# Retention's sample states weighted by their queries before a sum by ones, in units 2 to 7 of a decoder layer

## The chip, the cores and the metric

The kernel runs on one core of a Trainium2 chip. TensorE multiplies matrices, VectorE, ScalarE and GpSimd compute elementwise, and SyncE (SP) issues nearly all DMAs from one queue, in order. The metric is the device time of one execution in microseconds, 2566.4 as the median of three runs (2565.67 to 2569.12).

## The reference

One layer of a decoder trunk, for 16 + 256 prompt tokens and 8 sample tokens (one new token for each of eight sequences with states from the past): a SwiGLU half step, a mixer of Retention (8 heads of 256 by 256) and HGRN2 (16 heads of 128 by 128) behind one input projection of ten parts, an output projection, and a second half step. What the change touches is Retention's output for the sample tokens:

```python
def retention_chunk(S, q, k, v):          # C = 1 for a sample
    ...
    q_dec = q * jnp.exp(lg[:, None] * (idx + 1.0))[:, :, None].astype(q.dtype)
    o = jnp.einsum('bhij,bhjv->bhiv', inner, v) + jnp.einsum('bhid,bhdv->bhiv', q_dec, S)
    ...
    S_new = jnp.exp(lg * C)[:, None, None].astype(S.dtype) * S + jnp.einsum('bhjd,bhjv->bhdv', k_dec, v)
```

For one token, gamma times S plus k times v is the new state, and the output is the query times that new state. So for each head and each of the eight samples b, `o[b, :] = sum over d of q[b, d] * S_new[b, d, :]`, with d over 256, which the kernel holds as two halves c of 128 partitions.

## The kernel before

All matmuls with weights are written three times in fp32r (high by high, low by high, high by low) by `dense` (L218). `stream` loads 512 KB of weights into `raw` (L185, on SP), ScalarE rounds them to `whi` (L188), VectorE subtracts to get `wlo` (L189); each has three buffers of eight weight blocks. TensorE's instructions keep the order in which the program writes them. The other engines' orders are planned ahead by a scheduler that fills them by priority and readiness; after that every queue runs in its order.

The mixer runs over eight units u (a Retention head and two HGRN2 heads each). `project` makes the unit's six parts f, q_h, i_h, q_r, k_r, v_r, then the four gate groups of the unit before. A group is 16 steps k of six matmuls. After each step the hook calls `pump`, which counts down every waiting thread by one and lets those at zero run to their next `yield n`. So a unit has 160 steps, and a thread's position is counted in pumps.

- `mix_hg(u)` starts 4 pumps after i_h. It works off the decay levels (tiles K, Q, T, Qm), updates the sample states (`smh`), and for u of 2 or more waits 45 pumps, until pump 91 of its count, for its query matmuls (`pq`, L1039). After 7 pumps more come `outputs(0)`, then twice 10 for the two norms.
- `mix_ret(u)` starts 3 pumps after v_r, which is 48 pumps after i_h. `load(0)` and `load(1)` (L1095) fetch the states of samples 0 to 3 and 4 to 7 (e = 0, 1), two halves c each, in four buffers with the tag `smr`, which the tiles ks and vs share. `alone(qdr, q)` (L734) spreads the eight queries over a zeroed tile so that a 32-column weight holds one query. L1192 and L1198 update the states in place, L1202 writes them out. At pump 43 the visit of TensorE comes: `scores` for the last prompt tokens, then 16 matmuls (L1211) over e, c and the four column tiles j into `pq` (named pqr). 7 pumps later follow the two output matmuls (`por`), one pump each, and 12 pumps after the last of them the norm's sums (`pvr`), at pump 64.

Pump 43 of `mix_ret` and pump 91 of `mix_hg` are the same pump, so both visits follow each other.

`gate_groups(u)` come after the next unit's parts. The evacuation of a gate (`evacuate`, L690 to L705) calls `pump` without any dense step until the norm of its unit is done (`done_r`, `done_h`). For the last unit its own gate groups come right after those of unit 6: the first of them ends 80 pumps after v_r.

`st` is the dictionary through which `evacuate` hands tiles to the threads. `qdr` is a tile of 4 x 129 columns that holds nothing but Retention's queries.

Of the kernel before, what the change touches and what calls it, by code (L numbers as in the profile page):

```python
# [13 lines left out]
AF = mybir.ActivationFunctionType  # L14
ALU = mybir.AluOpType
# [8 lines left out]
NMETA, SEQ, NS = 16, 256, 8  # L24
# [104 lines left out]
def trunk(ctx: ExitStack, tc: tile.TileContext, A, O):  # L129
    nc = tc.nc  # L130
# [108 lines left out]
    def mul(out, a, b):  # L239
        nc.vector.tensor_tensor(out=out, in0=a, in1=b, op=ALU.mult)  # L240
# [306 lines left out]
    with tc.tile_pool(name="yp", bufs=1) as yp:  # L547
# [7 lines left out]
        with tc.tile_pool(name="mp", bufs=1) as mp:  # L555
# [28 lines left out]
            st = {}  # L584
# [7 lines left out]
            nc.gpsimd.memset(qdr, 0.0)  # L592
            qdh_at = [qdh.rearrange("p a c -> p (a c)")[:, 256 * h :] for h in range(2)]
            qdr_at = [qdr.rearrange("p a c -> p (a c)")[:, 2 * ALONE * c :] for c in range(2)]
            vsm = tmp("vsm", (P, P))
# [52 lines left out]
            def evacuate(n, c0, c1, o0, o1, b0, b1):  # L648
# [38 lines left out]
                elif n in ("g_r", "g_h"):  # L687
# [4 lines left out]
                    sa = tmp("gs", (P, TL), bufs=2)  # L692
                    nc.scalar.activation(sa, o1, AF.Sigmoid)
                    mul(t, t, sa)
                    u, e = divmod(c0, 2)
# [50 lines left out]
            def mix_hg(u, f, k, q, v):  # L746

                calm = 2
# [282 lines left out]
                if u == 1:  # L1031
                    yield 2
                    samples(1)
                yield (8, 11, 45)[min(u, 2)]
                pq = mx_bank("pq")
# [49 lines left out]
            def mix_ret(u, q, k, v):  # L1085
# [6 lines left out]
                def load(e):  # L1092
                    for c in range(2):
                        sms.append(tmp("smr", (P, 4, 256), bufs=4))
                        nc.sync.dma_start(sms[2 * e + c], A["sr"][u, c, :, 4 * e : 4 * e + 4, :])  # L1095

# [7 lines left out]
                for c in range(2):  # L1104
# [27 lines left out]
                    yield 2  # L1132
                alone(qdr, q)
                vts = [vt[:, 0], vt[:, 1], vs2]
# [54 lines left out]
                for e in range(2):  # L1189
# [13 lines left out]
                    yield 1 if e else 10 if u == 0 else 6  # L1203
                yield (11 if u == 0 else 15) + 2 * calm
                pq = mx_bank("pqr")
                scores(pq[:, 256:], 2)
                for e in range(2):
                    for c in range(2):
                        for j in range(4):
                            b = 4 * e + j  # L1210
                            nc.tensor.matmul(  # L1211
                                pq[32 * j : 32 * j + 32, :256], qdr_at[c][:, 32 * b : 32 * b + 32],
                                sms[2 * e + c][:, j, :], start=e + c == 0, stop=e + c == 2, tile_position=(0, 32 * j))
                mul(scr2[:NB2], pq[:NB2, 256 : 256 + NMETA], dt[:NB2, c2:])
# [162 lines left out]
```

## Time and profile before

| what | value |
|---|---|
| median of three runs | 2566.4 us (2565.67 to 2569.12) |
| span of the profiled execution | 2563.9 us |
| TensorE's granted clock in it | 1.000 |
| one unit, from the first pj_f of unit 3 to that of unit 4 in the windows view | 126.3 us |
| VectorE busy in that unit | 98.5 us |
| ScalarE busy in that unit | 84.7 us |
| GpSimd busy in that unit | 6.2 us |
| state loads `smr` from issue to landing, median | 5.0 us |
| weight loads of the input projection, median | 4.3 us |

The span runs from the first to the last instruction; the time of a run lies a little above it. Busy time of an engine is the union of its instructions. A row of a group says the line of the source, the engine, the operation, the tiles (out, then in), the shape and the count, then busy time and the mean duration of one, then the idle time ahead of them and what ended it. A row of the timeline begins with the start and the duration in us. A row of the tile view has the shortest, median and longest duration in ns after the count. A row of the waits view says who waited for whom: total, times, longest.

### The profile page before, as it was taken

To read this page: it belongs to the slowest core of one execution; us is meant where nothing else is said; L and a number is where in the kernel's file an instruction comes from. 1 tells how busy PE (TensorE), PEld (TensorE's weight loads), DVE (VectorE), ACT (ScalarE), POOL (GpSimd) and SP (SyncE) were. 2 spreads that over 40 slices of the span, in tenths; PEclk is the share of its full clock that TensorE was granted. 3 is DMA by queue.
4 is the path that set the end of the run, shared out by engine and by line. 5 is a ranking of instruction groups with operands and counts; after the bars stand their busy time and mean duration, and the time that the engine had idled before them with its cause. 6 is when DMAs were issued, how large, how long until landed. Compare 5 with 4: busy or idle time off the path is not lost.

```text
span 2563.9 us, 56275 instructions
## 1 busy us (share of the span) xinstructions
PE 2553.4 (100%) x23424; PEld 2534.4 (99%) x23424; DVE 1702.8 (66%) x2827; ACT 1392.2 (54%) x2186; POOL 57.0 (2%) x152
## 2 busy tenths in 40 slices
PE   9999999999999999999999999999999999999999
PEld 9999999999999999999999999999999999999998
DVE  6444544475569878777777777777885555556555
ACT  5444444444456767767676666675564444444443
POOL 0000000000000000000000000000000000000000
PEclk9999999999999999999999999999999999999999
DMA  7555555555555876767676767675556565565554
GB/s 244 183 187 183 187 182 184 186 182 186 184 201 180 287 265 232 264 214 260 212 264 215 259 223 255 224 239 188 196 190 197 194 197 195 194 196 195 195 195 149
DMA packets 156897, 536.26 MB, mean 209 GB/s; under 512 B 17952, under 2 KB 25952, under 8 KB 156640
## 3 DMA queue, kind: packets, MB, share of 16 engines
q1 hardware_dynamic: 156352, 532.37, 62.0%
q8 instruction: 183, 3.00, 0.5%
q14 instruction: 74, 0.61, 0.1%
q10 hardware_dynamic: 288, 0.29, 0.0%
HBM read 501.99 MB, written 30.61 MB: 208 GB/s over the span
## 4 chain that ended last, share of the span: by engine, by line
PE 96%; DVE 2%; ACT 0%; issue 0%; DMA 0%; SPq 0%; ACTq 0%; DVEq 0%
PE up L218 36%; PE dn L218 19%; PE pj_i_h L218 3%; PE pj_g_r L218 3%; PE pj_q_h L218 3%; PE pj_g_h L218 3%; PE pj_a_r L218 3%; PE pj_a_h L218 3%; PE pj_f L218 3%; PE pj_q_r L218 3%; PE pj_k_r L218 3%; PE wo L218 3%; PE pj_v_r L218 3%; DVE wlo L189 1%; PE pqr L1211 1%; PE psr L1168 0%
## 5 line engine op out<-in xcount | busy, mean ns | idle before, releaser
L189 DVE TENSOR_TENSOR wlo<-raw,whi 128x1024 fp32r<-128x1024 f32 (+1 forms) x869 | 1062.2, 1223 | 740.7 <-ACT whi L188 737.3
L188 ACT CAST whi<-raw 128x1024 fp32r<-128x1024 f32 (+1 forms) x870 | 905.7, 1042 | 909.2 <-PE up L218 411.0
L218 PE MATMUL up<-xh,whi 128*128 128x280 f32 (+1 forms) x2624 | 725.6, 280 | 0.6 <-ACT whi L188 0.6
L218 PE MATMUL up<-xh,wlo 128*128 128x280 f32 (+1 forms) x2624 | 725.8, 280 | 0.4 <-DVE wlo L189 0.3
L218 PE MATMUL up<-xl,whi 128*128 128x280 f32 (+1 forms) x2624 | 725.4, 279 | 0.0
L218 PEld LDWEIGHTS up<-xh,wlo 128*128 128x128 f32 x2624 | 492.6, 189 | 1.0 <-DVE wlo L189 1.0
L218 PEld LDWEIGHTS up<-xh,whi 128*128 128x128 f32 x2624 | 492.6, 189 | 0.8 <-ACT whi L188 0.8
L218 PEld LDWEIGHTS up<-xl,whi 128*128 128x128 f32 x2624 | 492.6, 189 | 0.0
L218 PE MATMUL dn<-hh,whi 128*128 128x280 f32 (+1 forms) x1376 | 384.7, 280 | 0.0
L218 PE MATMUL dn<-hh,wlo 128*128 128x280 f32 (+1 forms) x1376 | 384.3, 279 | 0.0
L218 PE MATMUL dn<-hl,whi 128*128 128x280 f32 (+1 forms) x1376 | 384.3, 279 | 0.0
L218 PEld LDWEIGHTS dn<-hh,whi 128*128 128x128 f32 x1376 | 260.1, 189 | 0.1
L218 PEld LDWEIGHTS dn<-hl,whi 128*128 128x128 f32 x1376 | 260.1, 189 | 0.1
L218 PEld LDWEIGHTS dn<-hh,wlo 128*128 128x128 f32 x1376 | 260.1, 189 | 0.0
L218 PE MATMUL pj_k_r<-xh,whi 128*128 128x280 f32 x256 | 74.2, 290 | 0.0
L218 PE MATMUL pj_g_r<-xh,whi 128*128 128x264 f32 x256 | 74.0, 289 | 0.0
L218 PE MATMUL pj_v_r<-xh,whi 128*128 128x280 f32 x256 | 73.8, 288 | 0.0
L218 PE MATMUL pj_v_r<-xh,wlo 128*128 128x280 f32 x256 | 72.4, 283 | 0.3 <-DVE wlo L189 0.3
L218 PE MATMUL pj_g_h<-xh,whi 128*128 128x264 f32 x256 | 72.7, 284 | 0.0
L218 PE MATMUL pj_k_r<-xh,wlo 128*128 128x280 f32 x256 | 72.4, 283 | 0.0
L218 PE MATMUL pj_v_r<-xl,whi 128*128 128x280 f32 x256 | 72.3, 283 | 0.0
L218 PE MATMUL pj_k_r<-xl,whi 128*128 128x280 f32 x256 | 72.3, 283 | 0.0
(421 smaller groups left out, 5263.4 us busy)
## 6 DMA issues: line engine op xcount, KB each, us to landing
raw<-in_w_up SPq DMA_DIRECT2D x343, 512.0 KB, 4.1
raw<-in_w_in SPq DMA_DIRECT2D x320, 512.0 KB, 4.3
raw<-in_w_dn SPq DMA_DIRECT2D x172, 512.0 KB, 3.5
smr<-in_sr SPq DMA_DIRECT2D x32, 512.0 KB, 5.0
out_srs<-smr SPq DMA_DIRECT2D x32, 512.0 KB, 6.7
raw<-in_w_out SPq DMA_DIRECT2D x32, 512.0 KB, 3.9
vbr<-vrd SPq DMA_DIRECT2D x32, 256.0 KB, 4.1
smh<-in_sg SPq DMA_DIRECT2D x16, 512.0 KB, 5.2
```

The costliest lines, as they stand in the source:

```text
L188: nc.scalar.copy(hi[:, j:jn, :], raw[:, j:jn, :])
L189: nc.vector.tensor_tensor(out=lo[:, j0:j1, :], in0=raw[:, j0:j1, :], in1=hi[:, j0:j1, :].bitcast(F32), op=ALU.subtract)
L218: nc.tensor.matmul(o, w, t, start=start, stop=stop)
L1211: nc.tensor.matmul(pq[32 * j : 32 * j + 32, :256], qdr_at[c][:, 32 * b : 32 * b + 32], sms[2 * e + c][:, j, :], start=e + c == 0, stop=e + ...
```

## The change

In units 2 to 7 the states are multiplied by the queries outside TensorE: for each sample b and the halves c, `s0 = s0 * q0`, then `s0 = s1 * q1 + s0`, per partition. The matmul then sums over the partitions with a weight of 32 columns in which one column is 1 (`one`), so the loop over c runs once. `one` and `late_q`, the eight queries of both halves, lie in `qdr`. The products for e = 0 are made on GpSimd, those for e = 1 on ScalarE, and the second step of both on VectorE. A GpSimd copy of one column of `st["seen"]`, the sigmoid of the gate evacuated last, stands ahead of the copy of the queries. The products are issued at pump 49 of `mix_ret` and the visit at pump 65; the wait in `mix_hg` grows from 45 to 67. The first two state loads of units 2 to 7 get a GpSimd copy ahead of them that reads a column of `st["q"]`, the HGRN2 queries of the unit, and writes into the buffer. Units 0 and 1 stay as they were.

```diff
+            one = qdr[:, 0, :64].rearrange("p (e m) -> p e m", e=2)
+            late_q = qdr[:, 1, : 2 * NS].rearrange("p (c b) -> p c b", c=2)
...
                     nc.scalar.activation(sa, o1, AF.Sigmoid)
+                    st["seen"] = sa
...
-                yield (8, 11, 45)[min(u, 2)]
+                yield (8, 11, 67)[min(u, 2)]
...
                         sms.append(tmp("smr", (P, 4, 256), bufs=4))
+                        if e == 0 and u > 1:
+                            nc.gpsimd.tensor_copy(sms[c][:, 0, :1], st["q"][:, 0, :1])
                         nc.sync.dma_start(sms[2 * e + c], A["sr"][u, c, :, 4 * e : 4 * e + 4, :])
...
-                alone(qdr, q)
+                if u < 2:
+                    alone(qdr, q)
...
-                yield (11 if u == 0 else 15) + 2 * calm
+                yield (11 if u == 0 else 15) + 2 * calm if u < 2 else 25
+                if u == 2:
+                    nc.gpsimd.memset(qdr[:, 0, :64], 0.0)
+                    for e in range(2):
+                        nc.gpsimd.memset(one[:, e, e : e + 1], 1.0)
+                if u > 1:
+                    nc.gpsimd.tensor_copy(late_q[:, 0, :1], st["seen"][:, :1])
+                    nc.gpsimd.tensor_copy(late_q, q[:, :, SEQ:])
+                    for e in range(2):
+                        s0, s1 = sms[2 * e : 2 * e + 2]
+                        for b in range(4):
+                            g = [late_q[:, c, 4 * e + b : 4 * e + b + 1] for c in range(2)]
+                            if e:
+                                nc.scalar.activation(s0[:, b, :], s0[:, b, :], AF.Copy, scale=g[0])
+                            else:
+                                nc.gpsimd.tensor_scalar(out=s0[:, b, :], in0=s0[:, b, :], scalar1=g[0], scalar2=None, op0=ALU.mult)
+                            nc.vector.scalar_tensor_tensor(
+                                out=s0[:, b, :], in0=s1[:, b, :], scalar=g[1], in1=s0[:, b, :], op0=ALU.mult, op1=ALU.add)
+                    yield 16
                 pq = mx_bank("pqr")
                 scores(pq[:, 256:], 2)
                 for e in range(2):
-                    for c in range(2):
+                    for c in range(2 if u < 2 else 1):
                         for j in range(4):
                             b = 4 * e + j
                             nc.tensor.matmul(
-                                pq[32 * j : 32 * j + 32, :256], qdr_at[c][:, 32 * b : 32 * b + 32],
-                                sms[2 * e + c][:, j, :], start=e + c == 0, stop=e + c == 2, tile_position=(0, 32 * j))
+                                pq[32 * j : 32 * j + 32, :256], qdr_at[c][:, 32 * b : 32 * b + 32] if u < 2 else one[:, e, :],
+                                sms[2 * e + c][:, j, :], start=e + c == 0, stop=e + c == 2 if u < 2 else e == 1, tile_position=(0, 32 * j))
```

## The prediction, made before the changed kernel ran

> **What bounds the kernel now.** I read the page's engine totals first, then the chain that ended last, then TensorE's waits.
>
> ```profile
> span 2563.9 us, 56275 instructions
> ...
> PE 2553.4 (100%) x23424; PEld 2534.4 (99%) x23424; DVE 1702.8 (66%) x2827; ACT 1392.2 (54%) x2186; POOL 57.0 (2%) x152
> ...
> PE 96%; DVE 2%; ACT 0%; issue 0%; DMA 0%; SPq 0%; ACTq 0%; DVEq 0%
> ...
> PE pw L515 <- DVE eps_h L163: 1.0, 1, 1.0
> PE pt L1116 <- POOL tails L1103: 0.9, 1, 0.9
> PE pj_f L218 <- DVE wlo L189: 0.7, 1, 0.7
> ```
>
> The reader is to see that TensorE is the chain (96%), and that its longest single wait on another engine is 1.0 us. Busy alone proves little, since matmuls are pipelined; the three rows of the waits view prove it. So a matmul that goes is time that goes, and any wait that is put into TensorE's queue is time that comes, one for one.
>
> **What goes: half of the query matmuls of units 2 to 7.** These rows are TensorE's timeline at the visit of unit 5 (start, duration, engine, line), and then the grouped row for all eight units.
>
> ```profile
> 1444.27 0.42 PE L1211 MATMUL pqr<-smr,qdr 128*32 128x256 f32 x3
> ...
> 1444.32 1.89 PE L1211 MATMUL pqr<-smr,qdr 128*32 128x256 f32 x29
> 1446.14 0.38 PE L218 MATMUL pj_g_r<-xh,whi 128*128 128x264 f32 x1
> ...
> 1445.59 0.40 PE L1211 MATMUL pqr<-smr,qdr 128*32 128x256 f32 x4
> ...
> 1445.81 0.40 PE L1211 MATMUL pqr<-smr,qdr 128*32 128x256 f32 x4
> ...
> L1211 PE MATMUL pqr<-smr,qdr 128*32 128x256 f32 x256 | 15.5, 381 | 0.0
> ```
>
> A unit has 16 matmuls of L1211 in the source and 32 records (256 / 8): float32 goes through twice. The four column tiles run side by side, so records start in groups of four. The first group's four start between 1444.27 and 1444.32, the eighth's at 1445.81: seven steps of 0.213 to 0.220 us, and I take 0.216 (the two rows of four alone give 0.22). The mean of 381 ns is therefore not the price; the step is. With the loop over c cut to one pass, 4 of 8 groups go: 4 x 0.216 = 0.86 us a unit, and 6 units make **5.2 us**. What surrounds the groups stays: the scores, the gap of about 0.3 us before the next dense matmul (1445.81 to 1446.14), and the float32 weights of 32 columns, which have the same shape whether they hold queries or ones. A cruder reading bounds it from below: 32 starts in 1.56 us are 0.050 us each, 16 of them 0.80 us, 4.8 us in all.
>
> **What comes, part by part.** Per unit: two small GpSimd copies (one waits for the gate's sigmoid), four GpSimd products of 128x256, four ScalarE products, eight VectorE folds; VectorE's small copy of the queries (L734) goes. They are issued 49 pumps after v_r, and the matmuls that read them at 65, where they were issued at 43. One pump is one k step of a projection.
>
> ```profile
> L1198 DVE SCALAR_TENSOR_TENSOR smr<-vbr,k_r,smr x64: 459/479/494, 839.5 to 1683.5; 128x256 f32<-128x256 f32 x64
> L998 ACT ACTIVATE smh<-smh,meta x128: 384/387/410, 866.7 to 1661.7; 128x128 f32<-128x128 f32 x128
> L1192 ACT ACTIVATE smr<-smr,gam x16: 1132/1147/1152, 838.2 to 1677.8; 128x1024 f32<-128x1024 f32 x16
> ...
> L1174 POOL TENSOR_SCALAR gam<-sro x8: 280/1172/1307, 832.2 to 1675.5; 128x1 f32<-128x1 f32 x8
> L592 POOL MEMSET qdr<- 128x516 f32 x1 | 0.5, 532 | 0.0
> ...
> 1448.83 0.28 PE L218 MATMUL pj_a_r<-xh,wlo 128*128 128x264 f32 x1
> ...
> 1449.39 0.28 PE L218 MATMUL pj_a_r<-xl,whi 128*128 128x264 f32 x1
> ...
> 1450.70 0.39 ACT L693 ACTIVATE gs<-pj_a_r 128x264 f32<-128x264 f32 x1
> ...
> 1449.10:1460.60 11.50, 11.50 (x102) 11.40 (x101) 7.16 (x15) 6.47 (x14) 0.00 (x0) 1.00 0.81 289
> ...
> POOL meta L910 <- DVE T L240: 298.6, 5, 59.9
> ```
>
> The row with a colon in its first field is of the windows view: length, then busy us (count) of PE, PEld, DVE, ACT and POOL, the clock, the DMA share and GB/s.
>
> VectorE: 8 x 0.48 = 3.8 us. ScalarE: 128 columns take 0.39, 1024 take 1.15, so 256 take about 0.48 (estimate), 1.9 us in four. GpSimd has no product of this size in the trace. From below: 0.28 us, the shortest TENSOR_SCALAR, of one column. To it I add 256 columns at the memset's rate, 532 / 516 = 1.03 ns each, 0.26 us, and take **0.54 us**. From above: a memset only writes; a product at twice its rate would take 0.8 us, and the wait below comes on top.
>
> The room: the sigmoid that releases the copies ends at 1451.1, 1.6 us after its group's last step (the dense work after pump 43 begins at 1446.14; five steps of six matmuls, 0.56 / 5 = 0.112 us each by the two PE rows, end at 1449.5). From there to pump 65 there are 16 steps of 0.675 us and one of 0.71 us (280 columns for 264), 11.5 us; 9.9 us remain after the sigmoid. Two copies (0.2 us each), four products each followed by its fold, and the four other folds beside ScalarE's products need 0.4 + 4 x 0.54 + 8 x 0.48 = 6.4 us even in a row, with about four weight subtractions (wlo) of 1.2 us between them. VectorE was busy 7.16 of 11.5 us in this window (third pair), and the query tails that stand there move out. So I cost the added work at nothing on TensorE; its cover is those 17 dense steps.
>
> How far VectorE may fall behind is seen where nothing disturbs:
>
> ```profile
> 1733.74 1.05 ACT L188 CAST whi<-raw 128x1024 fp32r<-128x1024 f32 x1 [1.65 <-PE pj_a_h L218]
> ...
> 1734.82 1.23 DVE L189 TENSOR_TENSOR wlo<-raw,whi 128x1024 fp32r<-128x1024 f32 x1 [1.13 <-ACT whi L188]
> ```
>
> The cast starts when TensorE frees a buffer; the new pair is done 2.3 us later and is needed after two other buffers of 24 matmuls, 2 x 2.7 = 5.4 us. The lead is some 3 us, and a shorter delay is free.
>
> **What moves.** The HGRN2 visit was at 91 pumps of its own count and goes to 113, still in Retention's pump, so the merged visit and the tails keep their distances. They leave the gates and land in the first 28 steps of the next unit, where VectorE works off the HGRN2 levels:
>
> ```profile
> 1343.86 0.43 DVE L265 SCALAR_TENSOR_TENSOR rt<-rt,rv 128x264 f32<-128x264 f32 x1
> ...
> 1372.99 0.43 DVE L240 TENSOR_TENSOR Q<-Q,T 128x256 f32<-128x256 f32 x1 [0.47 <-ACT Qm L921]
> ...
> 1380.80 0.29 PE L825 MATMUL pl<-Qm,k 128*32 128x48 f32 x8
> ```
>
> The last level there ends at 1373.4; TensorE asks at 1380.8, 7.4 us later. Two norm chains of some five instructions at 0.43 us stood in that stretch; three will, with squares and splits: about 5 us more (estimate), inside the 7.4. Cost nothing; beyond 7.4 us it would be a wait at pl. The levels need the old Q free, and its last reader moves only to step 18, ahead of the queries at 32.
>
> The first two state loads of a unit now wait for a GpSimd copy that reads the HGRN2 queries. Queued behind them on SP are the weight loads:
>
> ```profile
> 1443.99 0.47 SPq L1202 DMA_DIRECT2D out_srs<-smr  x1
> ...
> 1446.22 1.67 SPq L1095 DMA_DIRECT2D smr<-in_sr  x2
> 1449.58 2.84 SPq L185 DMA_DIRECT2D raw<-in_w_in  x2
> ...
> 1443.00:1454.00 11.00, 11.00 (x138) 9.85 (x137) 7.42 (x16) 6.00 (x14) 0.00 (x0) 1.00 0.97 344
> ...
> 1361.00:1373.00 12.00, 12.00 (x104) 12.00 (x103) 9.53 (x17) 6.78 (x14) 0.00 (x0) 1.00 0.53 181
> ...
> 1363.48 0.42 DVE L240 TENSOR_TENSOR q<-q,pj_q_h 128x264 f32<-128x264 f32 x1
> ...
> 1424.06 2.19 ACT L1192 ACTIVATE smr<-smr,gam 128x1024 f32<-128x1024 f32 x2 [1.29 <-POOL gam L1174]
> ...
> out_srs<-smr SPq DMA_DIRECT2D x32, 512.0 KB, 6.7
> ```
>
> They move from a stretch with DMA at 0.97 to one at 0.53; the queries stand at 1363.9 and the states are first used at 1424.1, so 60 us hide the transfer. Should the copy be late, SP holds back weight loads; nothing but VectorE's work on q stands ahead of it. The in-place products also wait for the outgoing state, issued last at 1443.99; its median time to landing, 6.7 us, puts its landing at 1450.7, before the copies are released. GpSimd's queue behind the sigmoid wait is empty for long: its next copy, meta at L910, waits up to 59.9 us today. ScalarE's products wait for the second copy with weight casts queued behind; 3 us of lead cover that.
>
> In unit 7 nothing follows: the norm that stood at pump 64 would stand at 86, but the gate evacuation needs it at 80, so six pumps are forced there without dense work between.
>
> ```profile
> 1706.95 0.32 PE L741 MATMUL por<-ident,osr 128*128 128x128 f32 x1
> ...
> 1710.44 0.43 DVE L226 TENSOR_TENSOR rlo<-sqr,rhi 128x264 fp32r<-128x264 f32 x1
> ```
>
> The split that the norm's sums need ended 3.9 us after the transpose. The change leaves 7 steps, 4.7 us, and the HGRN2 norm's matmuls ahead of it: no wait; without that cover 3.9 us, once.
>
> **Sum.** 2563.9 - 5.2 = 2558.7 us of span. The median of the runs is 2566.4, 2.5 us above the span, so 2566.4 - 5.2 = **2561.2 us**, 0.20% faster. One measurement of this kernel tells about 0.2%, 5.13 us, from no change, so the full gain stands on that bound.
>
> **Rivals.**
> *GpSimd and VectorE exclude each other, and the visit comes too early (slower).* The timelines of unit 4 show it:
>
> ```profile
> 1296.51 1.18 POOL L1174 TENSOR_SCALAR gam<-sro 128x1 f32<-128x1 f32 x1 [9.91 <-ACT sro L1170]
> ...
> 1296.43 1.21 DVE L189 TENSOR_TENSOR wlo<-raw,whi 128x1024 fp32r<-128x1024 f32 x1
> ```
>
> A product of one column, which can take 0.28 us, ended when the subtraction running beside it ended. If all six GpSimd instructions wait so, the copies take 2 x 1.17 and the products at 0.8 us take 4 x 1.97; with one fold behind them that is 10.7 us against 9.9, and if ScalarE's folds queue behind, 3 x 0.48 more after the first: TensorE waits 0.8 to 2.2 us a unit. At 2.2 x 6 = 13.2 us the time is 2566.4 - 5.2 + 13.2 = 2574.4. It decides from a product of (9.9 - 2.3 - 0.5) / 4 = 1.8 us on, its wait included. Against it: about four subtractions fall into the window, not six, and most folds are shorter. [...] Chance 0.15.
>
> *VectorE falls behind by more than its lead in places.* Folds (3.8), subtractions (4.3 x 1.2 = 5.1), the gate's evacuation (three of 0.43) and 6 GpSimd instructions' time (2.6) fill 12.8 of 11.5 us, if they never overlap: 1.3 us over, inside the lead of 3, but a bunch of folds ahead of one subtraction can use it up. 0.2 to 0.9 us of wait a unit leaves 2562.4 to 2566.4, say 2564; unit 7's wait of up to 3.9 us falls in here. For it: VectorE is the second busiest engine. Chance 0.22.
>
> *The change doesn't shorten the visit:* the groups that remain are stretched or restarts eat them. 2566.4. Against it: the step of 0.216 us is even over all groups. Chance 0.04.
>
> **How the numbers follow.** The forecast has 0.56, and a case of a little more than the sum 0.03. The full gain, 5.18 us unrounded, lies on the 0.2% bound, so I give 0.33 of the 0.56 to faster and 0.23 to no change. Faster: 0.33 + 0.03 = 0.36. Within 0.2%: 0.23 + 0.22 + 0.04 = 0.49. Slower: 0.15. The range takes the forecast with the spread of the runs (2565.67 to 2569.12, about 1.5 us to a side), the second rival and the third: 2559.7 to 2567.0; the slower rival lies outside.
>
> **What would show it.** Right: 16 records of L1211 in units 2 to 7, four steps of 0.216 us, dense matmuls 2.2 us apart around the visit instead of 3.0, and no new row in TensorE's waits. The units' period, one pj_f to the next, falls by 0.86 us. Wrong: TensorE waiting for smr on VectorE at pqr (first rival), for wlo at pj_f or pj_g_h (second), for Qm at pl, or for rlo at pvr in unit 7; GpSimd products far over 0.54 us; SP held at L1095.

## The result: slower, and the profile after

| | before | after |
|---|---|---|
| median | 2567.76 us (4 runs, 2565.67 to 2569.96) | 2588.06 us (4 runs, 2583.32 to 2589.02) |
| ratio | 1 | 1.0077, 95% interval 1.0063 to 1.0091 |
| span of the profiled execution | 2563.9 us | 2581.5 us |
| first matmul of pj_f to first matmul of wo (the mixer) | 1015.7 us | 1033.1 us |

The profiled executions differ by 17.6 us, and all but 0.2 of it lies in the mixer. The medians differ by 20.3 us: the profiled execution of the changed kernel took 2583.32 us, the fastest of its four, so its trace shows somewhat less than the typical loss. These rows of the tile views (shortest, median and longest duration, then first and last start) give its two ends, before and after: 1760.7 - 745.0 and 1778.2 - 745.1.

```profile
L218 PE MATMUL pj_f<-xhg,whi x32: 283/283/283, 745.0 to 766.8; 128*128 128x282 f32 x32
L218 PE MATMUL wo<-yh,whi x256: 276/276/470, 1760.7 to 1848.5; 128*128 128x264 f32 x128
```

```profile
L218 PE MATMUL pj_f<-xhg,whi x32: 283/283/283, 745.1 to 766.9; 128*128 128x282 f32 x32
L218 PE MATMUL wo<-yh,whi x256: 276/276/470, 1778.2 to 1866.1; 128*128 128x264 f32 x128
```

**What went as forecast.** TensorE's timeline at the visit of unit 4 after the change (start, duration, engine, line, operation):

```profile
1340.97 0.28 PE L218 MATMUL pj_f<-xh,wlo 128*128 128x280 f32 x1
1341.18 1.08 PE L1042 MATMUL pq<-smh,qdh 128*32 128x128 f32 x32
...
1342.13 0.42 PE L1235 MATMUL pqr<-smr,qdr 128*32 128x256 f32 x3
...
1342.18 1.03 PE L1235 MATMUL pqr<-smr,qdr 128*32 128x256 f32 x13
1343.14 0.39 PE L218 MATMUL pj_f<-xh,whi 128*128 128x280 f32 x1
```

16 records where there were 32; from the last dense start to the next it is 1343.14 - 1340.97 = 2.17 us, where before it was 3.03. That is 0.86 us a unit, and nothing in this visit waits for `smr`.

**What came instead.** TensorE's waits after (total, times, longest):

```profile
PE pj_g_h L218 <- DVE wlo L189: 12.2, 6, 2.3
PE pt L881 <- POOL ends L754: 4.0, 5, 0.9
```

Neither row was there before. TensorE waits once a unit for weights in the gate group of HGRN2 (pj_g_h), and in five units for a GpSimd copy (`ends`) in the next unit's levels. Together they are 16.2 us of the 22.6 that came (17.4 more in the mixer, though 5.2 went). A stall costs more than its row: matmuls of 0.28 us start every 0.11 us, and the one ahead of a stall runs out alone, some 0.17 us more (below, 2.55 us from the start at 1333.76 to that at 1336.31, for a row of 2.27 and a step of 0.11). Some matmuls also ran at half rate behind a stall (granted clock 0.50 for 2.7 us in unit 4, last section). This is how the first wait arises, in the timelines of GpSimd, ScalarE, VectorE and TensorE in unit 4 (the bracket is the idle time before the instruction and what ended it):

```profile
1329.51 0.95 POOL L1216 COPY qdr<-gs 128x1 f32<-128x1 f32 x1 [25.97 <-ACT gs L695]
1330.52 0.30 POOL L1217 COPY qdr<-q_r 128x16 f32<-128x16 f32 x1
1330.92 3.68 POOL L1225 TENSOR_SCALAR smr<-smr,qdr 128x256 f32<-128x256 f32 x4
...
1330.85 1.71 ACT L1223 ACTIVATE smr<-smr,qdr 128x256 f32<-128x256 f32 x4 [1.40 <-POOL qdr L1217]
1332.46 1.98 ACT L188 CAST whi<-raw 128x1024 fp32r<-128x1024 f32 x2
...
1329.19 1.23 DVE L189 TENSOR_TENSOR wlo<-raw,whi 128x1024 fp32r<-128x1024 f32 x1 [0.97 <-ACT whi L188]
...
1331.87 0.69 DVE L1226 SCALAR_TENSOR_TENSOR smr<-smr,qdr 128x256 f32<-128x256 f32 x1 [1.11 <-POOL smr L1225]
...
1332.83 0.69 DVE L1226 SCALAR_TENSOR_TENSOR smr<-smr,qdr 128x256 f32<-128x256 f32 x1
1333.73 0.69 DVE L1226 SCALAR_TENSOR_TENSOR smr<-smr,qdr 128x256 f32<-128x256 f32 x1 [0.21 <-POOL smr L1225]
1334.63 0.49 DVE L1226 SCALAR_TENSOR_TENSOR smr<-smr,qdr 128x256 f32<-128x256 f32 x1 [0.20 <-POOL smr L1225]
1335.03 1.22 DVE L189 TENSOR_TENSOR wlo<-raw,whi 128x1024 fp32r<-128x1024 f32 x1
...
1333.76 0.28 PE L218 MATMUL pj_g_h<-xl,whi 128*128 128x264 f32 x1
1336.31 0.59 PE L218 MATMUL pj_g_h<-xh,wlo 128*128 128x264 f32 x1 [2.27 <-DVE wlo L189]
1336.69 0.43 PE L218 MATMUL pj_a_h<-xh,whi 128*128 128x264 f32 x1
1336.91 0.43 PE L218 MATMUL pj_a_h<-xl,whi 128*128 128x264 f32 x1
```

Read it from the bottom. TensorE stops for 2.27 us, until the subtraction that began at 1335.03. Ahead of that subtraction in VectorE's queue stood four folds, and each started just behind the end of a GpSimd product of 3.68 / 4 = 0.92 us. GpSimd had begun late: its first copy ran beside the subtraction of 1329.19 and ended just behind it, at 1330.46 against 1330.42. On the other side ScalarE stood still for 1.40 us until the query copy was done, with the cast that this subtraction needs (the first of the two from 1332.46, done at about 1333.5) behind its products. From 1333.5 to 1335.03 it was the folds alone that held the subtraction.

### The profile page after: what moved, and what is told of

The parts are those of the page before. It is cut to its first block, busy times and chain, and to the rows that moved or that the text cites. A ratio compares the mean times of both kernels' runs of the same rounds, so it can differ in the third digit from the quotient of the medians.

```text
span 2581.5 us, 56206 instructions
## 1 busy us (share of the span) xinstructions
PE 2553.5 (99%) x23328; PEld 2533.3 (98%) x23328; DVE 1723.2 (67%) x2869; ACT 1397.0 (54%) x2208; POOL 91.3 (4%) x203
## 4 chain that ended last, share of the span: by engine, by line
PE 80%; DVE 7%; DMA 4%; ACT 4%; issue 2%; POOL 1%; SPq 0%; ACTq 0%; DVEq 0%; POOLq 0%
PE up L218 36%; PE dn L218 19%; DMA raw<-in_w_in 3%; DVE wlo L189 3%; PE pj_k_r L218 3%; PE wo L218 3%; PE pj_v_r L218 3%; PE pj_f L218 3%; PE pj_q_r L218 2%; ACT whi L188 2%; PE pj_g_r L218 2%; PE pj_a_r L218 2%; PE pj_g_h L218 1%; PE pj_a_h L218 1%; PE pj_q_h L218 1%
## 5 line engine op out<-in xcount | busy, mean ns | idle before, releaser
L218 PE MATMUL pj_g_h<-xh,wlo 128*128 128x264 f32 x256 | 72.0, 281 | 12.2 <-DVE wlo L189 12.2
```

What stands on the lines that cost most here:

```text
L218: nc.tensor.matmul(o, w, t, start=start, stop=stop)
```

## The lead of the weights, before and after

For each `wlo` I take the end of the subtraction and the start of the first matmul that reads it; the distance is the lead of the weights (eight weight blocks to one subtraction, paired by counting back from the last one). Two pairs of the kernel before, unit 4, with a cast of ScalarE ahead of them:

```profile
1311.90 1.05 ACT L188 CAST whi<-raw 128x1024 fp32r<-128x1024 f32 x1 [2.19 <-DMA raw<-in_w_in]
...
1313.63 1.22 DVE L189 TENSOR_TENSOR wlo<-raw,whi 128x1024 fp32r<-128x1024 f32 x1
1315.09 0.28 PE L218 MATMUL pj_g_r<-xh,wlo 128*128 128x264 f32 x1
...
1324.50 1.23 DVE L189 TENSOR_TENSOR wlo<-raw,whi 128x1024 fp32r<-128x1024 f32 x1 [0.50 <-ACT whi L188]
1331.63 0.28 PE L218 MATMUL pj_g_h<-xh,wlo 128*128 128x264 f32 x1
```

The first pair has 1315.09 - 1314.85 = 0.24 us of lead, the second 1331.63 - 1325.73 = 5.90. In between lies the visit (1316.8 to 1319.8) and after it the outputs. While TensorE works on them it uses no weights, and the weights gain their lead again. The visit gives most of it: the first pair behind it already has 1320.81 - 1317.32 = 3.49 us. Ahead of the visit the casts waited for their loads (2.19 us above), which share SyncE's queue with the state transfers there. After the change the visit is gone from there, and the pair of 1329.19 has its first use at:

```profile
1330.90 0.28 PE L218 MATMUL pj_g_h<-xh,wlo 128*128 128x264 f32 x1
```

1330.90 - 1330.42 = 0.48 us, just when products and folds begin. The median lead over all `wlo` of pj_g_h in units 2 to 6 (40 pairs a kernel, each unit counted from its first pj_f to the next one's), for the kernels that follow:

| kernels | median lead at pj_g_h |
|---|---|
| before; half_alone | 4.00; 3.95 us |
| shift_alone; no_products; the changed kernel | 0.92; 0.89; 1.11 us |
| no_hold; products_on_ScalarE; spread_unpinned; paced_on_GpSimd | 0.98; 0.87; 1.20; 0.83 us |
| paced_HGRN2_at_45; paced_late; late_to_6; block_late | 2.01; 2.76; 2.78; 2.57 us |
| late_both | 0.92 us |

The split is clean: both visits left in the gates, about 4 us; HGRN2's left there, 2.0 to 2.8; both moved, about 1 us.

## The experiments

Ratios are to runs of the kernel before made beside each (15 to 29 runs, medians 2566.8 to 2567.7 us). "Mixer" is first pj_f to first wo in the profiled execution, against 1015.7 us before.

| run | median us | ratio, 95% interval | mixer |
|---|---|---|---|
| half_alone | 2562.11 | 0.9983 (0.9974 to 0.9992) | 1011.2 |
| shift_alone | 2569.20 | 1.0009 (1.0000 to 1.0018) | 1018.9 |
| no_products | 2569.26 | 1.0010 (1.0001 to 1.0019) | 1019.3 |
| products_on_ScalarE | 2575.34 | 1.0030 (1.0018 to 1.0042) | 1024.6 |
| no_hold | 2584.95 | 1.0073 (1.0058 to 1.0088) | 1033.6 |
| products_on_VectorE | 2578.10 | 1.0043 (1.0028 to 1.0058) | 1028.0 |
| VectorE_no_hold | 2573.11 | 1.0024 (1.0015 to 1.0034) | 1024.5 |
| ScalarE_no_hold | 2574.73 | 1.0032 (1.0021 to 1.0044) | 1029.9 |
| spread_unpinned | 2576.39 | 1.0037 (1.0023 to 1.0050) | 1025.3 |
| paced_on_GpSimd | 2570.59 | 1.0016 (1.0008 to 1.0025) | 1022.0 |
| paced_HGRN2_at_45 | 2581.21 | 1.0047 (1.0034 to 1.0061) | 1033.2 |
| paced_late | 2570.60 | 1.0012 (1.0004 to 1.0021) | 1017.5 |
| late_to_6 | 2566.85 | 0.9999 (0.9990 to 1.0007) | 1014.8 |
| block_late | 2585.11 | 1.0073 (1.0059 to 1.0087) | 1030.6 |
| late_both | 2566.95 | 0.9999 (0.9990 to 1.0008) | 1014.4 |

The mixer is that of one execution, which need not lie near the median: those of ScalarE_no_hold (2579.63 us) and paced_HGRN2_at_45 (2584.34) were the slowest of their kernels, that of paced_late (2567.60) lay 3.0 us below its median.

### The parts alone

**half_alone**: the kernel before, with the second half of the query product (c = 1) left out in units 2 to 7 and nothing else changed.

```diff
-                    for c in range(2):
+                    for c in range(2 if u < 2 else 1):
...
-                                sms[2 * e + c][:, j, :], start=e + c == 0, stop=e + c == 2, tile_position=(0, 32 * j))
+                                sms[2 * e + c][:, j, :], start=e + c == 0, stop=e + c == (2 if u < 2 else 1), tile_position=(0, 32 * j))
```

> The kernel before, with one edit: in units 2 to 7 the loop over c runs once, so that only the first half of each query and state enters the sample outputs of Retention (the second half is left out); nothing is multiplied ahead and nothing is moved. If the sum's gain is right (four groups of 0.216 us a unit), TensorE's visit of pq and pqr takes 2.17 us instead of 3.03 in units 2 to 7 and the time falls by 5.2 us, ratio 0.998. If part of the changed kernel's loss came from TensorE itself, the time does not fall by that.

Mixer -4.5 us and median -4.8. By TensorE's records, the starts that belong to pqr take 10.3 us for 15.4, which is the 5.1 to 5.2 of the sum; one wait of 0.5 us at pj_g_r and what it costs around it make the rest.

**shift_alone**: the kernel before, with both visits and their tails 22 pumps later.

```diff
-                yield (8, 11, 45)[min(u, 2)]
+                yield (8, 11, 67)[min(u, 2)]
...
-                yield (11 if u == 0 else 15) + 2 * calm
+                yield (11 if u == 0 else 15) + 2 * calm if u < 2 else 41
```

> The kernel before with only the waits changed: 67 for 45 in mix_hg and 41 for 19 in mix_ret, so that the visit and the tails stand 22 pumps later in units 2 to 7, as in the changed kernel. Theory: the tails push HGRN2's levels on VectorE back, ScalarE's copies of v stand behind the levels' copies, and the transpose of the ends waits for GpSimd as in the changed kernel, about 0.8 us a unit in five units, with no wait for wlo at pj_g_h; +4 us, ratio 1.0016. Rival: the tails are harmless and the wait for the ends comes from the products; ratio 1.000.

Mixer +3.3 us, median +2.3, with nothing added. TensorE's waits of this kernel that are new:

```profile
PE pj_g_h L218 <- DVE wlo L189: 1.1, 2, 0.8
PE pj_g_r L218 <- DVE wlo L189: 0.7, 1, 0.7
PE pt L878 <- POOL ends L751: 0.3, 1, 0.3
```

They come to 2.1 us, and to some 2.8 with 0.17 us around each of the four. The expected mechanism was missed: `ends` waits 0.3 us, not 4, and the weights, which were to cost nothing, make most of it. With nothing added, the lead at pj_g_h fell from 4.00 to 0.92 us. So the shift alone takes the lead away. It moves visit and tails together; no run moves one without the other.

**no_products**: the changed kernel without products and folds (the sum by ones then takes unweighted states).

> The changed kernel with the products and folds left out: the states are not weighted, so Retention's sample outputs lack the queries. The two GpSimd copies, the held loads, the later visit and the halved matmuls stay. Theory: the waits for wlo at pj_g_h (12.2 us in the changed kernel's profile) and the slow matmuls behind them go, the waits for the ends (4.0 us) stay: -5.2 + 4 = -1 us, ratio 0.9996. Rival: the waits for wlo come from the moved work or the held loads, and stay; ratio about 1.006.

```profile
PE pt L881 <- POOL ends L754: 3.9, 6, 0.9
PE pj_g_h L218 <- DVE wlo L189: 1.4, 3, 0.8
```

Mixer +3.6 us; the median (+2.3) lies between the two expectations. The wait for `ends` stands here without any product, and that for weights has nearly gone. By differences of the mixer, added in this order, the loss splits so: records -5.2, shift +3.3, hold and copies 3.6 + 5.2 - 3.3 = +5.5, products and folds 1033.1 - 1019.3 = +13.8; together +17.4. By differences of the medians it is about -5, +2, +5 and +18.

### The products on other engines, and the hold

**products_on_ScalarE**: the four products of e = 0 on ScalarE too. **products_on_VectorE**: all eight first products on VectorE.

```diff
-                            if e:
-                                nc.scalar.activation(s0[:, b, :], s0[:, b, :], AF.Copy, scale=g[0])
-                            else:
-                                nc.gpsimd.tensor_scalar(out=s0[:, b, :], in0=s0[:, b, :], scalar1=g[0], scalar2=None, op0=ALU.mult)
+                            nc.scalar.activation(s0[:, b, :], s0[:, b, :], AF.Copy, scale=g[0])
```

> The changed kernel with GpSimd's four products done by ScalarE, which then has eight in a row. [...] Rival (any row of products that stands ahead of a cast or a subtraction in an in-order queue takes up the lead): ScalarE's eight products hold the next cast by about 3 us and the wait at pj_g_h stays at 1 to 2 us a unit, ratio 1.003 to 1.008.

> The changed kernel with all eight first products on VectorE itself instead of GpSimd and ScalarE; hold, later visit and the two GpSimd copies stay. Theory: the loss at pj_g_h is waiting across engines inside in-order queues (VectorE's folds for GpSimd's products, ScalarE's products for GpSimd's copy), with a cast and a subtraction queued behind; VectorE's own work of 8 x 0.3 + 8 x 0.48 us fits. The wait for wlo at pj_g_h falls to about what it was without products, 1.4 us in all, ratio about 1.001. Rival: it is the amount of work on VectorE ahead of a subtraction, whoever makes the products; with 2.4 us more of it the waits are 2 us a unit as before, ratio 1.007.

TensorE's waits with the products on ScalarE:

```profile
PE pt L881 <- POOL ends L754: 4.3, 6, 0.9
PE pj_g_h L218 <- DVE wlo L189: 4.2, 7, 0.8
```

Without GpSimd's products the wait for weights falls from 12.2 to 4.2 us, the longest from 2.3 to 0.8: most of the wait at pj_g_h was VectorE standing in its queue for GpSimd. At 0.7 us a unit the rest lies between the under 0.5 that would be left if GpSimd's products held up the folds and nothing else did, and the rival's 1 to 2; that it is the work itself with a lead under 1 us is argued, not shown. On VectorE the same work gave waits at pqr for `smr` (2.5 us in six), pj_f (1.5, of which 0.7 was there before) and pj_g_h (1.3, as its theory said); there the visit came too early.

**no_hold**: the changed kernel without the copies ahead of the state loads.

```diff
-                        if e == 0 and u > 1:
-                            nc.gpsimd.tensor_copy(sms[c][:, 0, :1], st["q"][:, 0, :1])
```

> The changed kernel without the GpSimd copies that hold the first two state loads until the HGRN2 queries stand; all else as changed. Theory: the held loads put 1 MB ahead of the weight loads in the stretch of HGRN2's levels, a cast there waits for its weights and ScalarE's copies of v wait behind it, so the wait of the transpose for GpSimd's ends (4 us in all) goes without the hold, while the waits for wlo at pj_g_h stay: 2588 - 4 = 2584 us, ratio about 1.006. Rival: the moved tails cause the wait for the ends (it was 0.3 us with the shift alone, against this); then nothing changes, ratio 1.0077.

The wait for `ends` is gone but for 0.3 us, and next to nothing is gained: pj_g_h waits 13.6 us in eight, and some matmuls ran at half rate (clock 0.50 for 5.3 us in one stretch, below). What the hold does is seen in the changed kernel's ScalarE and GpSimd in unit 5:

```profile
1379.20 1.04 ACT L188 CAST whi<-raw 128x1024 fp32r<-128x1024 f32 x1 [1.67 <-DMA raw<-in_w_in]
...
1381.88 0.41 ACT L810 COPY Qm<-Q 128x256 f32<-128x256 f32 x1 [1.29 <-DVE Q L240]
...
1383.42 0.40 ACT L670 COPY v<-pj_i_h 128x280 f32<-128x280 f32 x1
...
1383.87 0.97 POOL L753 COPY ends<-v 128x32 f32<-128x32 f32 x1 [12.46 <-ACT v L670]
```

The cast waits 1.67 us for a weight load that shares SyncE's queue with the held state loads (DMA share 0.86 from 1371.3 to 1379.2); ScalarE's copies of v, behind it, come up to 3.0 us after the last matmul of i_h (started at 1380.38), and GpSimd's copy for `ends` after them. Between the two ScalarE also waited 1.29 us for VectorE's Q. That the hold makes the wait for `ends` is shown by its going here; the way from the cast to the copies is a reading of this one unit.

**VectorE_no_hold**, **ScalarE_no_hold**: all products and the query copy on the one engine, without the hold and without the copy that waits for the sigmoid.

> Products on VectorE as in the run before, and besides neither the hold of the state loads nor the copy that waits for the gate's sigmoid; the copy of the queries is made by VectorE. Theory: both sources of waiting are gone, so the 5.2 us of TensorE show, less the 3 us that the shift alone cost: ratio 0.999 to 1.000. Rival: without the sigmoid's hold the products are planned earlier, where VectorE is busy with the state updates, and waits for wlo come back there; ratio over 1.002.

> All first products and the copy of the queries on ScalarE, no hold of the state loads and no copy that waits for the sigmoid. Theory: the run with ScalarE's products lost 4.3 us to the ends and 4.7 us at pj_g_h; without the hold the first goes, without the wait for GpSimd's copy most of the second: ratio 0.999 to 1.001. Rival: eight products of 0.45 us in ScalarE's queue alone delay a cast by more than the lead; the wait at pj_g_h stays at 0.8 us a unit, ratio about 1.0015.

At most 0.3 us for `ends` in either. Weights: 7.6 us at pj_g_h in the first; 5.9 at pj_g_r (1.4 of it for whi) and 5.0 at pj_g_h (2.9 for whi) in the second. Both fall on the side of their rivals, ScalarE_no_hold beyond it. Without the sigmoid copy the planner moves the work forward (first product at 1062.3 and 1060.8 us against 1073.9), as VectorE_no_hold's rival said.

### Pacing and place

**spread_unpinned**: no hold, no sigmoid copy; products and folds written one per pump.

```diff
+                    half(0, 0, range(4))
+                    yield 1
+                    for b in range(4):
+                        half(1, 0, [b])
+                        yield 1
+                        half(1, 1, [b])
+                        yield 1
+                    for b in range(4):
+                        half(0, 1, [b])
+                        yield 1
+                    yield 3
```

> The changed kernel without the hold of its state loads and without the copy that waits for the sigmoid (the query copy goes to ScalarE); products and folds are written one per pump instead of all at pump 49, the visit stays at pump 65. Theory (the loss is that a run of folds or products stands ahead of a subtraction or cast in an in-order queue, and waits there for GpSimd): no fold waits for GpSimd, at most two stand together ahead of a subtraction, so VectorE's delays stay near 1 us; the waits for wlo and whi fall from the 14 us of the changed kernel to under 5, and the time lies between 2564 and 2570. Rival (VectorE and ScalarE simply have no room there for 8 folds and 4 products a unit, wherever they stand): waits near those of the other variants without the hold (7 to 9 us), 2573 to 2575.

Missed, since the pumps are only a priority: nothing ties the products to a pump, and the planner put them right behind the states' update. The group row of GpSimd's products and TensorE's wait:

```profile
L1226 POOL TENSOR_SCALAR smr<-smr,qdr 128x256 f32<-128x256 f32 x24 | 27.9, 1182 | 82.2 <-DMA out_srs<-smr 82.2
```

```profile
PE pj_g_r L218 <- DVE wlo L189: 7.9, 6, 2.6
```

GpSimd waited there for the outgoing state (82.2 us in all), the folds for GpSimd, the subtractions for the folds. The wait moved to pj_g_r; the theory's claim on order was not tested by it.

**paced_on_GpSimd**: no hold; all products on GpSimd, in pairs 4 pumps apart, the folds of a pair a step behind, each step tied to the weights in use by a copy of four of their columns.

```diff
+                    for m in range(5):
+                        w = late_q[:, m, :]
+                        nc.gpsimd.tensor_copy(w, block.state["hi"][:, 0, :4].bitcast(F32))
...
+                                nc.gpsimd.tensor_scalar(out=s0[:, b, :], in0=s0[:, b, :], scalar1=w[:, i : i + 1], scalar2=None, op0=ALU.mult)
...
+                                nc.vector.scalar_tensor_tensor(
+                                    out=s0[:, b, :], in0=s1[:, b, :], scalar=w[:, 2 + i : 3 + i], in1=s0[:, b, :], op0=ALU.mult, op1=ALU.add)
+                        yield 4
```

> The changed kernel without the hold; all eight products on GpSimd, two at a time, 4 pumps apart from pump 49, and the two folds of a pair 4 pumps after its products, each step tied to the weights then in use by a GpSimd copy of four of their columns; the visit at pump 69. ScalarE gets nothing. Theory (waiting in the queue, not the work, is the loss): products are done when their folds come, VectorE loses at most two folds, 1 us, ahead of any subtraction; waits for wlo under 4 us in all, none for smr; 2563 to 2568, so no slower than before. Rival (weights arrive with so little lead here that each 1 us of folds shows on TensorE): a stall of 0.5 to 1 us per pair, 2 to 3 us a unit, 2572 to 2578.

TensorE's waits for weights, and VectorE's folds waiting for GpSimd's small copies:

```profile
PE pj_g_h L219 <- DVE wlo L189: 2.8, 8, 0.7
PE pj_g_r L219 <- DVE wlo L189: 2.1, 4, 0.9
```

```profile
DVE smr L1229 <- POOL qdr L1226: 17.7, 23, 2.5
```

From 1.0073 (no_hold) to 1.0016 with more work on GpSimd than there, and stalls of under 1 us stay, with a lead of still 0.83 us. That lies between the two forecasts. The waiting in the queue does not go: the folds wait 17.7 us here, against 9.2 for GpSimd's products in no_hold. What goes are the runs: the folds come in pairs, with subtractions between the pairs. So the waiting alone does not set the loss; how much waiting and work stands ahead of one subtraction does, as far as these two runs tell.

**paced_HGRN2_at_45**: the same, HGRN2's visit back at its old place.

> paced_on_GpSimd with the wait in mix_hg back at 45 pumps, so that only Retention's visit is late (pump 69). The sum so far: 2567.0 before, 5.2 off for the records, some 3 on for the shift of both tails (shift_alone, 2.3 by its median), some 5 on for the folds. If HGRN2's share of the shift is what costs, 2567 to 2569; if Retention's tail or the folds cost it, no change: 2570 to 2572.

Both expectations missed, at 2581.2 us. At pj_g_h 1.2 us of waits are left, but HGRN2's and Retention's tails now queue at other points: `ends` 4.7 us, the copies of v 1.6, the norm's hlo at pv 1.9, and rhi at pvr in unit 7 2.0. So `ends` can also be late without the hold.

**paced_late**: as that, and in units 2 to 6 everything of Retention's 16 pumps later, in the next unit's f and q_h.

```diff
-                yield (11 if u == 0 else 15) + 2 * calm if u < 2 else 25
+                yield (11 if u == 0 else 15) + 2 * calm if u < 2 else 41 if u < 7 else 25
```

> As that, and in units 2 to 6 the products, folds and visit of Retention another 16 pumps later (products from pump 65, visit at 85), in the next unit's f and q_h, where the DMA share is 0.4 to 0.7 and not 1.0. Theory (folds cost because weights arrive with no lead behind the state transfers of the gates): the waits for wlo at pj_g_r and pj_g_h fall to those of half_alone (0.5 us), none takes their place at pj_f and pj_q_h, 2563 to 2566, faster than before. Rival (VectorE, 7.1 of 7.9 us busy at the levels, is as full there): waits for wlo at pj_f, pj_q_h or pj_i_h of 0.5 to 1 us a unit, or waits for Qm at pl, 2568 to 2573.

Waits at pj_g_r of 1.1 us in two, none new at pj_f or pj_q_h. Units 4 to 6 take 125.8 to 126.0 us from pj_f to pj_f, unit 3 126.9 (the next expectation counts unit 3 among them, wrongly); before it was 126.3. In unit 7, which has no next unit, pvr waits 2.0 us. The waits are nearer to the theory, but the median, 2570.60, lies in the range of the rival and equals that of paced_on_GpSimd.

**late_to_6** leaves unit 7 as it was before. **block_late** is the changed kernel's own block, all at one pump, at the same late place. The two differ in the pacing and, with it, in the visit's pump (85 and 81) and in the engine of e = 1.

```diff
+                new = 1 < u < 7
...
+                yield (11 if u == 0 else 15) + 2 * calm if not new else 41
```

> paced_late with unit 7 as in the kernel before (no products, 32 records, visit at pump 43). In paced_late units 3 to 6 took 125.9 to 126.0 us a unit against 126.33 before, and what was left over lay in unit 7, a wait of 2.0 us at pvr among it. Theory (the added work is free behind the gates, the loss there was where it stood; unit 7 has no such place): the wait at pvr goes, 0.3 to 0.5 us a unit stay, 2563.5 to 2566, faster than before by 1 to 3 us. Rival (a visit that crosses into the next unit costs about what it saves): 2567 to 2570.

> The changed kernel's own block (four products on GpSimd, four on ScalarE, eight folds, all at one pump) without the hold, at the later place of late_to_6: pump 65, visit at 81, units 2 to 6 alone, mix_hg at 45. It differs from late_to_6 in the pacing alone. If the place is what counts, 2563.5 to 2567 like late_to_6; if a run of folds that waits for GpSimd costs wherever it stands, waits for wlo at pj_f or pj_q_h of 1 to 2 us a unit, 2572 to 2578.

late_to_6 equals the kernel before, between its two expectations; block_late is slower than either of its own. late_to_6 has this as its only wait in the gates; block_late has these two:

```profile
PE pj_g_r L219 <- DVE wlo L189: 0.6, 2, 0.4
```

```profile
PE por L744 <- DVE osr L1086: 9.0, 5, 2.3
PE pj_q_h L218 <- DVE wlo L189: 4.3, 5, 0.9
```

In block_late's timelines, unit 4, the folds show the same picture as in the changed kernel:

```profile
1346.26 4.92 POOL L1226 TENSOR_SCALAR smr<-smr,qdr 128x256 f32<-128x256 f32 x4
...
1347.22 0.69 DVE L1227 SCALAR_TENSOR_TENSOR smr<-smr,qdr 128x256 f32<-128x256 f32 x1 [1.11 <-POOL smr L1226]
...
1351.21 2.07 DVE L1227 SCALAR_TENSOR_TENSOR smr<-smr,qdr 128x256 f32<-128x256 f32 x5 [0.21 <-POOL smr L1226]
...
1360.24 1.05 ACT L188 CAST whi<-raw 128x1024 fp32r<-128x1024 f32 x1 [1.31 <-DMA raw<-in_w_in]
1361.19 0.36 ACT L1242 COPY osr<-pqr 128x256 f32<-128x256 f32 x1
...
1364.18 0.30 PE L744 MATMUL por<-ident,osr 128*128 128x128 f32 x1 [2.31 <-DVE osr L1086]
```

Folds wait for GpSimd, and the weights queued behind are late by 0.9 us. Retention's own centred output (`osr`) is late by 2.3 us: its copy on ScalarE stood behind a cast that waited 1.31 us for its load, and on VectorE it stood behind HGRN2's norm and four subtractions. How much of these 9.0 us comes from the folds, and how much from a visit that is four pumps earlier, no run separates. So the later place alone cures nothing for the block. That the place is needed beside the pacing is not shown: paced_on_GpSimd and paced_late have one median, and late_to_6 also leaves unit 7 out.

**late_both**: late_to_6 with HGRN2's visit moved along, so that both stand together.

```diff
-                yield (8, 11, 45)[min(u, 2)]
+                yield (8, 11, 87 if u < 7 else 45)[min(u, 2)]
```

> late_to_6 with mix_hg's query visit also 42 pumps later in units 2 to 6 (87 for 45), so that both visits stand together again. In late_to_6 they stand apart: 1.43 + 1.50 us from dense to dense, where the changed kernel's joint visit takes 2.40, so 0.53 us a unit is lost, 2.7 us in all. If HGRN2's tail costs nothing that late: 2564 to 2565, faster than before by 2 to 3 us. If it does (its tail now runs up to the next unit's levels, whose buffers it shares): a wait for HGRN2's tiles at pl, pt or psc, 2567 or more.

The joint visit does take 2.38 us again (1.43 + 1.50 when split, each up to the second dense start), and units 5 and 6 take 125.5 us, as units 4 and 6 of half_alone. But the split cost less than the expectation says: its two windows hold two dense steps of 0.11 us more than the joint one, so it costs 2.93 - 2.38 - 0.22 = 0.33 us a unit, 1.6 in five, not 2.7. And the lead at pj_g_h fell from 2.78 to 0.92 us, the waits for `wlo` at pj_g_r and pj_g_h rose from 0.6 to 1.8 us, and the median did not move; the waits came for weights, not for HGRN2's tiles. No version that does the whole computation beat the kernel before; late_to_6 and late_both equal it.

## Why the prediction was wrong

The forecast was 2561.2 us and faster; it came out at 2588.1, slower than the slower rival too.

- **The records (5.2 us): right.** 2.17 us around the visit, no wait there, and half_alone gains 4.8 us.
- **The step that failed: "The lead is some 3 us, and a shorter delay is free."** I read it at 1733.74 in unit 7 of the kernel before, behind its visit, where it is right (3.2 us), and applied it to a stretch from which the change removes the visit. Before, the lead was 0.2 us ahead of the visit and up to 5.9 behind it. The visit and the outputs made the lead, and the change takes them away where it adds the work (shift_alone: 4.00 to 0.92 us). In its place the runs show 0.48 us in unit 4 and a median of 1.11, so what VectorE is late beyond that comes out on TensorE: up to 2.3 us a unit, 12.2 in six.
- **"So I cost the added work at nothing on TensorE": 13.8 us.** The sum of 6.4 us in a row against 9.9 us of cover was made against the visit. But the visit was not what asked first; the next `wlo` was. Room in a window is no answer where another instruction stands in the queue. TensorE never waited for `smr`.
- **GpSimd's product at 0.54 us, bounded by 0.8: mis-sized.** It took 0.92, also where nothing of VectorE ran beside it (unit 2's first, 0.926). The memset at 1.03 ns a column was no near row for an operation that also reads. Four folds stood in VectorE's queue for these products, ahead of a subtraction; with the products on ScalarE the wait at pj_g_h fell from 12.2 to 4.2 us.
- **"Cost nothing" for the shift of the tails: +3.3 us** by shift_alone's mixer, +2.3 by its median, for visit and tails together. I looked only for what the tails delay in the next unit, and not for what their absence does to the gates. The slack at pl held: no wait at pl.
- **The held loads, "60 us hide the transfer": true for the transfer, wrong for its neighbours.** The states came in time; the weight loads beside them came late (a cast waited 1.67 us for one at 1379.20 in unit 5). Hold and copies cost 5.5 us with no product (no_products), yet taking the hold alone out of the changed kernel gains 0.04%, inside the intervals: the waits for weights at pj_g_h grow from 12.2 to 13.6 us, and two stalls instead of one are followed by half rate (clock 0.50 in the longest). I cannot say more of its separate price.
- **ScalarE: "3 us of lead cover that" fell with the lead.** ScalarE waited 1.40 us for GpSimd's copy with casts behind it.
- **Unit 7: no wait at pvr in the changed kernel, as forecast**, but one of the six for weights, 2.27 us at 1725.98. The 2.0 us at pvr appear in paced_late and paced_HGRN2_at_45, where the pacing ends four pumps later.
- **The rivals.** VectorE falling behind its lead was the right mechanism, at the named place, with the wrong size: 0.2 to 0.9 us a unit against 2.0 (12.2 us in 6). It was sized against 3 us of lead as well (and 0.9 us in six units is 5.4, so its range ends at 2566.6). The exclusion of GpSimd and VectorE was half there: the first copy ended with the subtraction (1330.46 and 1330.42), as forecast, but TensorE did not wait at pqr.

What stays open: the mixer's rest in late_to_6, -0.9 us where 5 units should give -4.3. Of the 3.4 us that are missing, 1.6 are the split visit, 0.9 the waits (0.6 at pj_g_r, 0.3 for `ends`) and some 0.5 the time around these three stalls; about 0.4 is left. In late_both 3.0 us are missing, of which the waits are 2.0 (1.8 for weights, 0.2 for `ends`) and the time around the four stalls some 0.7; about 0.3 is left. Open too is what the products cost at a place with 4 us of lead: no run keeps both the old visit and the products.

## What to carry to other kernels

Before moving a block of matmuls that needs no new weights, ask what it gives the weight stream: a pause of TensorE is where loads, casts and subtractions gained their lead here (0.24 us ahead of the visit, 3.49 behind it), and the lead must be read at the place and after the move, not in a calm stretch. Cost added work on an in-order engine by the next instruction behind it that TensorE needs, and by what that work itself waits for, not by the room up to its own consumer. Work that waits for a slower engine goes into a queue only in small pieces, with the urgent work between them (paced_on_GpSimd against no_hold: 1.0016 for 1.0073).

## What the runs showed of the hardware

**Half rate after a stall.** After the 2.27 us of unit 4 the matmuls start 0.22 us apart (1336.69, 1336.91 above), not 0.11. The windows view of the changed kernel (columns as in the prediction; the granted clock follows the busy times):

```profile
1336.60:1339.30 2.70, 2.70 (x13) 2.70 (x13) 2.70 (x6) 0.00 (x0) 0.00 (x0) 0.50 0.58 193
1330.00:1333.00 3.00, 3.00 (x29) 3.00 (x28) 1.89 (x5) 2.15 (x5) 2.84 (x5) 1.00 0.76 247
```

The granted clock is 0.50 for 2.7 us, which costs some 1.3 us more (an estimate: 12 steps of 0.22 us from 1336.69 to 1339.33, for 0.11). Of six stalls of 1.7 to 2.3 us in this execution one had it. Behind the other five the clock is 1.00, with 23 matmuls in some 2.65 us, though two of them lasted 2.27 us as well (to 1597.03 and 1725.98). In no_hold two had it, the longer for 5.3 us (1340.5 to 1345.8, 26 matmuls, clock 0.50). So the length of the stall alone does not decide it, and what does, no run shows. Such a stall of 2.3 us can cost 3.6 (2.3 + 1.3) and in no_hold some 5 (2.3 + 2.7), an estimate from these windows.

**GpSimd and VectorE side by side.** In the changed kernel a fold beside a GpSimd product took 0.69 us, alone 0.48; the product took 0.92 either way. GpSimd's first copy took 0.95 us beside a subtraction that ended with it (1330.46 and 1330.42 in unit 4); copies of one column took 0.20 to 0.47 us in the mean in the kernel before. The fold of 1331.87 did not end with its neighbour: it ended at 1332.56, while the product that started at 1331.84 (1330.92 + 0.92) ran to 1332.76. In block_late four products took 4.92 us, for 3.68 in the changed kernel, where a subtraction of 1.21 us (1348.23) ran beside them. Why the fold is slowed and not stopped, no run shows.
